# One factor of a state space layer, B a^r, made with the states on partitions and turned by TensorE; the loads of that layer put in another order

## The chip, the cores and the metric

The kernel runs on one core of a Trainium2 chip. The metric is device time in microseconds of one execution. Before the change three runs took 1512.39, 1514.38 and 1520.98 us, so the median is 1514.38 us.

## The reference

The program is a trunk of four residual layers on 256 tokens of 1024 channels, all in float32. Each layer is a token mixer, then cross-attention (4 heads) into 256 memory tokens, then a gated MLP (d_ff 2816) with a causal convolution of width 3. Layers 0 and 3 mix by trailing-window means, layer 1 by stick-breaking attention, layer 2 by a diagonal complex state space (64 groups of 16 channels, 64 complex states each) followed by a GLU. The part that matters here, cut:

```python
def s5_mixer(h, a_re, a_im, log_dt, b_re, b_im, c_re, c_im, d, w_glu):
    lam = lax.complex(a_re, a_im)
    dt = jnp.exp(log_dt)[:, None]
    a_bar = jnp.exp(lam * dt)
    b_bar = ((a_bar - 1.0) / lam)[..., None] * lax.complex(b_re, b_im)
    ...
    bu = jnp.einsum('bcgi,gpi->bcgp', u_blk, b_bar)          # u = rms_norm(h)
    xs = scan over the 256 tokens: x_t = a_bar x_{t-1} + bu_t
    y = jnp.real(jnp.einsum('bcgp,gip->bcgi', xs, c_mat)) + d * u
    val, gate = jnp.split(gelu(y) @ w_glu, 2, axis=-1)
    return val * sigmoid(gate)
```

## The kernel before, in words

All big products are three float32r matmuls on a high and a low part of each operand (`mm3`, L65 to L67). A weight tile of 1 MB is loaded on SyncE's queue into one of three `raw` buffers (L88), rounded to its high part `whi` by ScalarE (L70), and its rest `wlo` is formed by VectorE (L71), or by GpSimd where asked for. The MLP takes 22 chunks of 128 columns (`up0` to `up21`): 48 matmuls into `u`, the convolution on ScalarE and VectorE (L1251, L1253), a gate, and 12 matmuls into four accumulators `acc`, two chunks late.

The state space layer cuts the 256 tokens into 32 chunks of 8. It needs three tables that depend on parameters alone, and these are made long before layer 2, in gaps of earlier layers: `B a^r` for r = 0..7, by which eight inputs become one chunk's contribution to the state (`blD`, 8 blocks m of 128 x 1024, in DRAM); `C a^r`, by which a carried state becomes eight outputs (`caD`); and the taps inside a chunk, `C a^r B` (`tD`). In layer 2, `u` (the normed input) is reshuffled by eight DMAs into `uc` with the chunks on partitions, copied into `ur` in another order, transposed by TensorE into `v`, and multiplied with `bl` (from `blD`) into `S`. `S` is transposed to `SX`, VectorE scans over the chunks into `X` (L1053 to L1066), and TensorE adds the taps (`tu` from `tD`, L1078) and the carried states (`ou` from `caD`, L1098) into `Y`. After a GELU come the GLU's products. Between these steps stand units of the cross-attention's projections of the memory, k1, k2, k3, v0 and v1, which do not depend on the layer's input.

How `B a^r` is made before: `s5_rows` (L801) orders the powers `pr`, `pi` and the matrix `bb` on GpSimd, transposes them on TensorE and writes them as rows to DRAM (`pwD`, `bbD`) from ScalarE's queue. `s5_rows_in` (L832) reads for each block m one row for 16 partitions (powers) or 8 (matrix), twice 512 KB, on GpSimd's queue. `s5_ba` (L839) makes the complex product in six VectorE operations on 128 x 512 elements, already in the layout of `blD`, and GpSimd's queue writes the block. Blocks 0 to 4 stand in the MLP of layer 0 (chunks up7 to up21), blocks 5 to 7 in the stick-breaking attention of layer 1 (its heads 3 to 13), where all three write the same half of a tile `s5o`.

What sets the order: the code is written with `fill("name")` points; `run` puts pieces of other work there with `put` and `plan`. The build then orders each engine's instructions by its own schedule, under the data dependences and the `behind(...)` constraints. Each engine takes its instructions in that order, and one that waits holds up all behind it; each DMA queue is issued in order as well.

Of the kernel before, what the change touches and what calls it, by code (L numbers as in the profile page):

```python
# [8 lines left out]
F32 = mybir.dt.float32  # L9
# [5 lines left out]
P = 128  # L15
# [21 lines left out]
class Trunk:  # L37
# [684 lines left out]
    def s5_start(self):  # L722

        nc, v, a = self.nc, self.nc.vector, self.a
# [64 lines left out]

        self.pwD = self.dram.tile([8, 8, 1024], F32, name="pwD")  # L790
        self.bbD = self.dram.tile([8, 16, 1024], F32, name="bbD")
# [9 lines left out]
    def s5_rows(self, after):  # L801

        nc = self.nc
        pr, pi, bb, C, t1, t4, t5, t6 = self.s5p
        jobs = []
        for x, y in enumerate((pr, pi)):

            src = t4[:, 1536 + 256 * x : 1792 + 256 * x]
            with self.behind(*after):
                nc.gpsimd.tensor_copy(src.rearrange("p (m k q) -> p m k q", m=8, k=8), y[:, 0:8, :].rearrange("p k (q m) -> p m k q", m=8))  # L810
            jobs += [(src[:, h * P : (h + 1) * P], self.pwD[4 * h : 4 * h + 4], x) for h in range(2)]
        for x in range(2):

            src = t6[:, 512 * x : 512 * (x + 1)]
            bv = bb.rearrange("p (q m) x j -> p m x j q", m=8)[:, :, x]
            with self.behind(*after):
                nc.gpsimd.tensor_copy(src.rearrange("p (m j q) -> p m j q", m=8, j=16), bv)
            jobs += [(src[:, h * P : (h + 1) * P], self.bbD[2 * h : 2 * h + 2], x) for h in range(4)]
        for b in range(3):
            ps = self.bank()  # L820
            for i in range(4):
                src = jobs[4 * b + i][0]
                nc.tensor.transpose(ps[:, i * P : (i + 1) * P], src, self.ident[:])
            st = t4[:, 512 * b : 512 * (b + 1)]
            nc.scalar.copy(st, ps[:])
            for i in range(4):
                _, dst, x = jobs[4 * b + i]
                nc.scalar.dma_start(
                    dst.rearrange("m k (x q p) -> x (m k) q p", x=2, q=4)[x], st[:, i * P : (i + 1) * P]
                )  # L830

    def s5_rows_in(self, m, t):  # L832

        nc = self.nc
        w, b = self.pwD[m], self.bbD[m]
        nc.gpsimd.dma_start(t[:, 0:1024], bass.AP(tensor=w.tensor, offset=w.offset, ap=[[1024, 8], [0, 16], [1, 1024]]))
        nc.gpsimd.dma_start(t[:, 1024:2048], bass.AP(tensor=b.tensor, offset=b.offset, ap=[[0, 8], [1024, 16], [1, 1024]]))

    def s5_ba(self, m, t, of, tmp, x):  # L839

        v = self.nc.vector
        f = lambda t: t.rearrange("p (x q k) -> p x q k", x=2, q=4)
        w, b = f(t[:, 0:1024]), f(t[:, 1024:2048])
        o = of.rearrange("p (q x k) -> p q x k", q=4, x=2)
        tmp = tmp.rearrange("p (q k) -> p q k", q=4)
        v.tensor_mul(o[:, :, x], w[:, 0], b[:, x])
        v.tensor_mul(tmp, w[:, 1], b[:, 1 - x])
        (v.tensor_add if x else v.tensor_sub)(o[:, :, x], o[:, :, x], tmp)
        if x:
            self.nc.gpsimd.dma_start(self.blD[:, m, :], of)  # L850

    def s5_tiles(self, m):

        pr, pi, bb, C, t1, t4, t5, t6 = self.s5p
        return (t5 if m % 2 else t4), (t1 if m % 2 else t6)[:, 0:1024], t6[:, 1280:1792]

    def s5_tiles_later(self, m):

        if self.s5r is None:
            self.s5r = [self.kv.tile([P, 2048], F32, tag=t, name="s5r") for t in ("mgh", "mgl")]  # L860
            self.s5r.append(self.big.tile([P, 2048], F32, tag="xs", name="s5o"))
        o = self.s5r[2]
        return self.s5r[m % 2], o[:, 0:1024], o[:, 1024:1536]
# [75 lines left out]
    def s5_mixer(self, l, sp):  # L939
# [10 lines left out]
        land(1)  # L950
# [6 lines left out]
        chain, firsts, last = [], [None, None], None  # L957
        for tt in range(TT):
            r = rs[tt]
            for nh, f in enumerate((nc.vector.tensor_scalar_mul, nc.scalar.mul)):  # L960
                s = slice(512 * nh, 512 * (nh + 1))
                done = f(u[:, tt, s], self.h[:, tt, s], r[:, 0:1])
                firsts = firsts[1:] + [done.ins]

                for q in (2 * nh, 2 * nh + 1):
                    at = 32 * q + 16 * tt
                    queue = nc.scalar if nh else nc.sync
                    moved = queue.dma_start(
                        uc[at : at + 16].rearrange("c t a j -> c t (a j)"), u[:, tt, 256 * q : 256 * (q + 1)]
                    )  # L970
                    last = last if nh else moved
# [5 lines left out]
        db = sp.tile([P, 2, 256], F32, name="db")  # L977
        for i, row in enumerate((a["s5_d"][0], a["mix_norm_g"][l])):
            for q in range(4):
# [444 lines left out]
```

## Time and profile before

| what | value |
|---|---|
| median of the runs | 1514.38 us |
| the profiled execution: its time, its span | 1520.19 us, 1518.5 us |
| PE busy | 1440.2 us, 95% of the span |
| MLP of layer 0 | about 143 to 353 us |
| stick-breaking attention of layer 1 (projections and heads) | about 353 to 488 us |
| MLP of layer 1 | about 611 to 809 us |
| state space layer | about 809 to 950 us |
| MLP of layer 2, of layer 3 | about 1021 to 1209, 1320 to 1508 us |

TensorE is busy nearly always, so what the change is worth is read from the stretches where it is not, or where its clock was lowered, and from the instructions that it gains. The places that it touches are the MLP of layer 0, the attention of layer 1 and the state space layer.

### The profile page before, as it was taken

The numbers are of one execution on the slowest core, as the hardware profiler recorded it, in microseconds if no ns is written. First come the engines' busy times: TensorE is split into PE (matmuls) and PEld (weight loads), VectorE is DVE, ScalarE is ACT, GpSimd is POOL, SyncE is SP. The second block draws the span as 40 slices with busy tenths as digits, with TensorE's granted clock in tenths as the row PEclk, the third lists the DMA queues.
The fourth block names the chain that finished last, engine by engine and source line by source line (L and its number), as shares of the span: only waits on it lengthen the run. The fifth ranks groups of instructions, "written<-read, shape, count | busy, mean of one in ns | idle before, by whom it ended". The sixth has DMA issues, their size and how long they took to land.

```text
span 1518.5 us, 25333 instructions
## 1 busy us (share of the span) xinstructions
PE 1440.2 (95%) x10318; PEld 1324.3 (87%) x10318; DVE 1096.0 (72%) x1720; ACT 833.4 (55%) x1338; POOL 139.6 (9%) x148
## 2 busy tenths in 40 slices
PE   7999998899899999999997779999999999999997
PEld 7898997798898998999986667989999999899996
DVE  6868677678787666998874755768777686677775
ACT  6554543465677455655544334656555575465553
POOL 3401000000000000011113420000000030000000
PEclk9999999999899999999998889999999999999999
DMA  7567898655543555676577575536564455365551
GB/s 251 202 182 222 230 260 226 203 169 177 156 139 112 165 182 175 226 240 224 194 245 214 206 266 180 181 111 222 187 202 167 155 196 190 113 224 190 169 192 43
DMA packets 211737, 288.10 MB, mean 190 GB/s; under 512 B 26340, under 2 KB 167268, under 8 KB 209700
## 3 DMA queue, kind: packets, MB, share of 16 engines
q1 hardware_dynamic: 198820, 261.74, 52.5%
q0 software_dynamic: 10496, 23.43, 5.8%
q10 hardware_dynamic: 2304, 1.31, 0.4%
q8 instruction: 81, 1.33, 0.4%
q14 instruction: 36, 0.29, 0.1%
HBM read 271.81 MB, written 17.73 MB: 191 GB/s over the span
## 4 chain that ended last, share of the span: by engine, by line
PE 77%; DVE 10%; DMA 8%; issue 2%; ACT 2%; ACTq 0%; SPq 0%; POOL 0%; DVEq 0%; POOLq 0%
PE u L65 9%; PE u L66 9%; PE u L67 9%; PE mm L65 7%; PE acc L67 7%; PE acc L66 7%; PE mm L66 7%; PE acc L65 7%; PE mm L67 7%; DMA raw<-in_ffn_w_up_dram 4%; DVE wlo L71 3%; DVE ug L1253 1%; DMA raw<-in_xa_wkv_dram 1%; PE z L551 1%; DMA blD<-s5o 1%
## 5 line engine op out<-in xcount | busy, mean ns | idle before, releaser
L71 DVE TENSOR_TENSOR wlo<-raw,whi 128x1024 fp32r<-128x1024 f32 x428 | 517.8, 1221 | 181.0 <-ACT whi L70 163.0
L70 ACT CAST whi<-raw 128x1024 fp32r<-128x1024 f32 (+1 forms) x450 | 458.7, 1045 | 231.1 <-DMA raw<-in_ffn_w_up_dram 99.4
L65 PE MATMUL u<-ah,whi 128*128 128x256 f32 x1408 | 400.2, 284 | 2.9 <-DVE ug L1253 2.2
L67 PE MATMUL u<-ah,wlo 128*128 128x256 f32 x1408 | 399.8, 284 | 1.4 <-DVE wlo L71 1.4
L66 PE MATMUL u<-al,whi 128*128 128x256 f32 x1408 | 399.8, 284 | 0.2 <-DVE al L71 0.2
L65 PEld LDWEIGHTS u<-ah,whi 128*128 128x128 f32 x1408 | 271.2, 193 | 7.9 <-issue 3.6
L66 PEld LDWEIGHTS u<-al,whi 128*128 128x128 f32 x1408 | 271.2, 193 | 3.4 <-DVE al L71 0.7
L67 PEld LDWEIGHTS u<-ah,wlo 128*128 128x128 f32 x1408 | 271.1, 193 | 2.0 <-DVE wlo L71 2.0
L1253 DVE SCALAR_TENSOR_TENSOR ug<-u,cwT,ug 128x255 f32<-128x255 f32 x352 | 168.1, 480 | 86.4 <-ACT ug L1251 81.8
L1251 ACT ACTIVATE ug<-u,cwT 128x256 f32<-128x256 f32 x176 | 99.0, 563 | 159.4 <-PE u L67 86.6
L65 PE MATMUL acc<-whi,gg 128*128 128x512 f32 x352 | 140.0, 398 | 11.2 <-ACT gg L70 11.0
L66 PE MATMUL acc<-wlo,gg 128*128 128x512 f32 x352 | 139.5, 396 | 0.0
L67 PE MATMUL acc<-whi,gg 128*128 128x512 f32 x352 | 138.6, 395 | 0.7 <-DVE gg L71 0.6
L66 PE MATMUL mm<-al,whi 128*128 128x256 f32 x384 | 110.0, 287 | 0.1
L65 PE MATMUL mm<-ah,whi 128*128 128x256 f32 x384 | 110.1, 287 | 0.0
L67 PE MATMUL mm<-ah,wlo 128*128 128x256 f32 x384 | 109.7, 286 | 0.0
L176 POOL TENSOR_TENSOR r<-v,mhalf 128x1 f32<-128x1 f32 x28 | 21.0, 751 | 842.0 <-DVE v L172 673.0
L65 PEld LDWEIGHTS acc<-whi,gg 128*128 128x128 f32 x352 | 67.2, 191 | 23.9 <-ACT gg L70 12.2
L67 PEld LDWEIGHTS acc<-whi,gg 128*128 128x128 f32 x352 | 67.0, 190 | 17.2 <-DVE gg L71 2.7
L66 PEld LDWEIGHTS acc<-wlo,gg 128*128 128x128 f32 x352 | 67.3, 191 | 11.0
L66 PEld LDWEIGHTS mm<-al,whi 128*128 128x128 f32 x384 | 74.8, 195 | 0.8 <-DVE al L71 0.6
L65 PEld LDWEIGHTS mm<-ah,whi 128*128 128x128 f32 x384 | 75.0, 195 | 0.1
(354 smaller groups left out, 2605.0 us busy)
## 6 DMA issues: line engine op xcount, KB each, us to landing
raw<-in_ffn_w_up_dram SPq DMA_DIRECT2D x88, 1024.0 KB
raw<-in_ffn_w_down_dram SPq DMA_DIRECT2D x44, 1024.0 KB
raw<-in_xa_wkv_dram SPq DMA_DIRECT2D x30, 1024.0 KB
raw<-in_xa_wq_dram SPq DMA_DIRECT2D x16, 1024.0 KB
raw<-in_xa_wo_dram SPq DMA_DIRECT2D x16, 1024.0 KB
raw<-in_sb_w_qkv_dram SPq DMA_DIRECT2D x12, 1024.0 KB
raw<-in_s_w_glu_dram SPq DMA_DIRECT2D x8, 1024.0 KB
raw<-in_sb_w_o_dram SPq DMA_DIRECT2D x4, 1024.0 KB
```

What stands on the lines that cost most here:

```text
L65: mm(out, lh, rh, start=start, stop=False)
L66: mm(out, lh, rl, start=False, stop=False)
L67: self.multiplied = mm(out, ll, rh, start=False, stop=stop).ins
L70: x = self.nc.scalar.copy(hi, src)
L71: y = (eng or self.nc.vector).tensor_sub(lo, src, hi.bitcast(F32))
L176: self.powed = nc.gpsimd.tensor_tensor(r[:], v[:], self.mhalf[:], ALU.pow).ins
L551: mm(out, qk[a][rows, 4 + qc, ks], qk[b][rows, qc, :], start=kt == 1 and n == 0, stop=False, skip_group_check=True)
L1251: nc.scalar.activation(u[:, s, :], out, AF.Identity, bias=cw[3], scale=cw[2])
L1253: nc.vector.scalar_tensor_tensor(u[:, s, sh:], out[:, : T - sh], cw[2 - sh], u[:, s, sh:], ALU.mult, ALU.add)
```

## The change

First, `B a^r`. `s5_rows` and `s5_rows_in`, the DRAM tables `pwD` and `bbD`, the twelve transposes that made them, their twelve DMA writes from ScalarE's queue, four GpSimd copies and the sixteen reads of 512 KB are gone. `s5_ba` makes the same six products with the states on partitions, out of `pr`, `pi` and `bb` where they lie, through broadcast access patterns. The new `s5_turn` transposes the result on TensorE (eight 128 x 128 transposes a block), ScalarE copies two PSUM banks of 128 x 512 to SBUF, and GpSimd's queue writes the block to `blD` as before. Since `pr`, `pi` and `bb` have left SBUF by layer 1, one load of 800 KB (`s5r<-keepD`, on SyncE's queue) brings them back for blocks 5 to 7. The transposed blocks of layer 1 now alternate between two halves of `s5o`.

Second, layer 2. Only `land(0)` stands ahead of the eight `uc` DMAs, which all go on SyncE's queue (before, four went on ScalarE's); the loads of `db` are two instead of eight and stand behind them, and so do `land(1)` and `land(2)`. `ur` is allocated ahead of `v`. The first quarter of the taps (`taps_u(0)`) stands ahead of v1, the other three, with their loads, behind it; the loads `ou` take other buffers.

```diff
-    def s5_rows(self, after):
...
-    def s5_rows_in(self, m, t):
...
+    def s5_ba(self, m, where, x):
+        v = self.nc.vector
+        (pr, pi, bb), o, tmp, _ = where
+        sh = [P, 4, 8, 16]
+        w = [y.rearrange("p k (q m) -> p m q k", m=8)[:, m, :, 0:8].unsqueeze(3).to_broadcast(sh) for y in (pr, pi)]
+        bv = bb.rearrange("p (q m) x j -> p m q x j", m=8)[:, m]
+        b = [bv[:, :, i, :].unsqueeze(2).to_broadcast(sh) for i in range(2)]
+        f = lambda t: t.rearrange("p (q r j) -> p q r j", q=4, r=8)
+        o = o.rearrange("p (q x k) -> p q x k", q=4, x=2)[:, :, x].rearrange("p q (r j) -> p q r j", r=8)
+        v.tensor_mul(o, w[0], b[x])
+        v.tensor_mul(f(tmp), w[1], b[1 - x])
+        (v.tensor_add if x else v.tensor_sub)(o, o, f(tmp))
+    def s5_turn(self, m, where):
+        _, o, _, of = where
+        for b in range(2):
+            ps = self.bank()
             for i in range(4):
+                s = slice(512 * b + P * i, 512 * b + P * (i + 1))
+                nc.tensor.transpose(ps[:, P * i : P * (i + 1)], o[:, s], self.ident[:])
+            nc.scalar.copy(of[:, 512 * b : 512 * (b + 1)], ps[:])
+        nc.gpsimd.dma_start(self.blD[:, m, :], of)
...
     def s5_tiles_later(self, m):
         if self.s5r is None:
+            k, t = [self.kv.tile([P, 2048], F32, tag=t, name="s5r") for t in ("mgh", "mgl")]
+            self.nc.sync.dma_start(k[:, 0:1600], self.keepD[:, 0:1600])
...
+        k3, o, tmp, of = self.s5r
+        return k3, o, tmp, of[:, 1024 * (m % 2) : 1024 * (m % 2) + 1024]
...
         land(0)
-        land(1)
...
-                for q in (2 * nh, 2 * nh + 1):
-                    at = 32 * q + 16 * tt
-                    queue = nc.scalar if nh else nc.sync
-                    moved = queue.dma_start(
...
+            for q in range(4):
+                at = 32 * q + 16 * tt
+                last = nc.sync.dma_start(
...
+        db = sp.tile([P, 2, 256], F32, name="db")
         with self.behind(last.ins):
+            for i, row in enumerate((a["s5_d"][0], a["mix_norm_g"][l])):
+                nc.sync.dma_start(db[:, i, :], bass.AP(tensor=row.tensor, offset=row.offset, ap=[[256, 4], [0, 32], [1, 256]]))
+            land(1)
             land(2)
...
-        v = self.acts.tile([P, 16, P], F32, tag="ah", name="v")
         ur = self.acts.tile([P, 16, 8, 16], F32, tag="ah", name="ur")
+        v = self.acts.tile([P, 16, P], F32, tag="ah", name="v")
...
+        taps_land(0)
...
         self.late = steps[-1:]
+        taps_u(0)
         self.fill("scan1")
         self.late = ()
+        for mm in (1, 2, 3):
+            landed = taps_land(mm)
+            taps_u(mm)
         def carry(mm):
-            pool, tag = ((self.big, "xs"), (self.acts, "ah"), (self.raw, "raw"), (self.raw, "raw"))[mm]
+            pool, tag = ((self.big, "xs"), (self.raw, "raw"), (self.raw, "raw"), (self.acts, "ah"))[mm]
...
+        for m in range(8):
+            l, tiles, at = (0, self.s5_tiles, [f"up{4 + 3 * m + i}" for i in range(3)])
+            if m > 4:
+                l, tiles, at = (1, self.s5_tiles_later, [f"head{1 + 4 * (m - 5) + i}" for i in (1, 2, 3)])
+            for x in range(2):
+                put((l, at[x]), lambda m=m, tiles=tiles, x=x: self.s5_ba(m, tiles(m), x))
+            put((l, at[2]), lambda m=m, tiles=tiles: self.s5_turn(m, tiles(m)))
+        put((1, "head0"), lambda: self.s5_tiles_later(5))
```

The schedule moves more than the diff shows. On VectorE, at the start of layer 1 (`al` is the normed input's low part, `s5o` and `s5r` belong to `B a^r`, `L` to the attention's first head), before:

```order
L71 TENSOR_TENSOR al<-mm,ah 128x4x128 x2
L846 TENSOR_TENSOR s5o<-s5r 128x4x128
L847 TENSOR_TENSOR s5o<-s5r 128x512
L846 TENSOR_TENSOR s5o<-s5r 128x4x128
L71 TENSOR_TENSOR wlo<-raw,whi 128x1024 x4
L71 TENSOR_TENSOR al<-mm,ah 128x512
L71 TENSOR_TENSOR wlo<-raw,whi 128x1024 x2
L848 TENSOR_TENSOR s5o<-s5o 128x4x128
L847 TENSOR_TENSOR s5o<-s5r 128x512
```

On the same engine at the same place, after the change:

```order
L71 TENSOR_TENSOR al<-mm,ah 128x4x128 x2
L71 TENSOR_TENSOR wlo<-raw,whi 128x1024 x4
L71 TENSOR_TENSOR al<-mm,ah 128x512
L71 TENSOR_TENSOR wlo<-raw,whi 128x1024 x4
L71 TENSOR_TENSOR al<-mm,ah 128x512
L558 TENSOR_SCALAR L<-z 128x384
L559 TENSOR_TENSOR L<-L,ab 128x384
```

No product of `B a^r` is left there: the six of block 5 stand in the last chunks of layer 0's MLP, the others further into the heads. Likewise the six of block 0 moved forward, into the norm ahead of layer 0's MLP, between the residual adds (L434) and the scaling of its second half (L248).

On SyncE's queue, from the load of k3's weights to the last load of `bl` (`db` is a small table for the skip term; lines of the change are some 26 lower):

```order
 L88 DMA raw<-in_xa_wkv_dram 128x8x256
-L980 DMA db<-in_s_d_dram 32x256 x4
-L980 DMA db<-in_mix_norm_g_dram 32x256 x4
-L946 DMA bl<-blD 128x2048
-L968 DMA uc<-u 16x8x256 x4
-L946 DMA bl<-blD 128x2048
+L922 DMA bl<-blD 128x2048
+L943 DMA uc<-u 16x8x256 x8
+L952 DMA db<-in_s_d_dram 128x1x256
+L952 DMA db<-in_mix_norm_g_dram 128x1x256
+L922 DMA bl<-blD 128x2048 x2
```

The load of `bl` that waited behind the eight of `db` now follows k3's weights directly; two loads of `bl` stand behind the `uc` DMAs instead of one.

On the same queue, from v0's weights to the GLU's:

```order
 L88 DMA raw<-in_xa_wkv_dram 128x4x512 x2
-L1074 DMA tu<-tD 128x2048 x4
+L998 DMA tu<-tD 128x2048
 L88 DMA raw<-in_xa_wkv_dram 128x4x512 x2
-L1090 DMA ou<-caD 128x2048 x4
-L88 DMA raw<-in_s_w_glu_dram 128x4x512
+L998 DMA tu<-tD 128x2048 x3
+L1076 DMA ou<-caD 128x2048 x4
+L88 DMA raw<-in_s_w_glu_dram 128x4x512 x3
```

Three of the four loads of taps moved behind v1's weights. The four `ou` stand in the order 0, 3, 1, 2: `ou` 3 takes the buffer of the first taps, and `ou` 1 and 2 take the `raw` buffers of the second and third taps, so they wait until TensorE has used those. Before, one GLU load came ahead of the next layer norm's row, now three do.

More of the change, by code (lines that the diff above doesn't have):

```diff
@@ L788, in s5_start @@
         self.blD = self.dram.tile([P, 8, 1024], F32, name="blD")
-        self.pwD = self.dram.tile([8, 8, 1024], F32, name="pwD")
-        self.bbD = self.dram.tile([8, 16, 1024], F32, name="bbD")
         self.caD = self.dram.tile([P, 8, 8, P], F32, name="caD")
@@ L799, in s5_start @@
         )
-    def s5_rows(self, after):
-        nc = self.nc
[L804 to L819, printed above, removed]
+    def s5_ba(self, m, where, x):
[10 more added lines that the diff above has]
+        (v.tensor_add if x else v.tensor_sub)(o, o, f(tmp))
@@ L820, in s5_rows @@
+    def s5_turn(self, m, where):
+        nc = self.nc
+        _, o, _, of = where
+        for b in range(2):
             ps = self.bank()
             for i in range(4):
[L822 to L830, printed above, removed]
@@ L832, in s5_rows_in @@
-    def s5_rows_in(self, m, t):
[L834 to L850, printed above, removed]
+                s = slice(512 * b + P * i, 512 * b + P * (i + 1))
@@ L859, in s5_tiles_later @@
         if self.s5r is None:
[L860 to L863, printed above, removed]
+            k, t = [self.kv.tile([P, 2048], F32, tag=t, name="s5r") for t in ("mgh", "mgl")]
+            self.nc.sync.dma_start(k[:, 0:1600], self.keepD[:, 0:1600])
+            f = lambda n: k[:, n : n + 288].rearrange("p (k g) -> p k g", k=9)
@@ L865, in s5_back @@
+            k3 = f(0), f(288), k[:, 576:1600].rearrange("p (g x j) -> p g x j", x=2, j=16)
+            self.s5r = k3, t[:, 0:1024], t[:, 1024:1536], self.big.tile([P, 2048], F32, tag="xs", name="s5o")
+        k3, o, tmp, of = self.s5r
+        return k3, o, tmp, of[:, 1024 * (m % 2) : 1024 * (m % 2) + 1024]
     def s5_back(self):
@@ L956, in s5_mixer @@
         uc = sp.tile([P, 8, 16, 16], F32, name="uc")
-        chain, firsts, last = [], [None, None], None
+        chain, firsts = [], []
         for tt in range(TT):
             r = rs[tt]
+            firsts = []
             for nh, f in enumerate((nc.vector.tensor_scalar_mul, nc.scalar.mul)):
@@ L1017, in s5_mixer, with taps_land @@
         self.fill("s")
+        tus = []
+        def taps_land(mm):
+            pool, tag = ((self.acts, "ah"), (self.raw, "raw"), (self.raw, "raw"), (self.raw, "raw"))[mm]
+            tu = pool.tile([P, 2, 2, 4, P], F32, tag=tag, name="tu")
+            tus.append(tu)
+            return nc.sync.dma_start(tu[:].rearrange("p r m q k -> p r (m q) k"), self.tD[mm]).ins
+        taps_land(0)
         SX = self.acts.tile([P, NCH, 2, GP], F32, tag="al", name="SX")
@@ L1068, in s5_mixer, with taps_u @@
         self.fill("scan0")
-        values = self.multiplied
         Y = self.accs()
-        for mm in range(4):
-            tu = self.raw.tile([P, 2, 2, 4, P], F32, tag="raw", name="tu")
-            landed = nc.sync.dma_start(tu[:].rearrange("p r m q k -> p r (m q) k"), self.tD[mm]).ins
-            with self.behind(values):
+        def taps_u(mm):
+            with self.behind(self.multiplied):
                 for m, par, q in [(m, par, q) for m in (2 * mm, 2 * mm + 1) for par in range(2) for q in range(4)]:
@@ L1332, in run @@
         put((0, "fnorm"), self.s5_start)
-        put((0, "up3"), lambda: self.s5_rows(self.transposed_all))
-        early = lambda m, x: self.s5_ba(m, *self.s5_tiles(m), x)
-        for m in range(2):
-            put((0, f"up{4 + m}"), lambda m=m: self.s5_rows_in(m, self.s5_tiles(m)[0]))
-        for m in range(5):
-            at = 7 + 3 * m
-            put((0, f"up{at}"), lambda m=m: early(m, 0))
-            put((0, f"up{at + 1}"), lambda m=m: early(m, 1))
-            if m < 3:
-                put((0, f"up{at + 2}"), lambda m=m: self.s5_rows_in(m + 2, self.s5_tiles(m)[0]))
-        later = lambda m, x: self.s5_ba(m, *self.s5_tiles_later(m), x)
-        for m in (5, 6, 7):
-            at = 3 + 4 * (m - 5)
-            put((1, f"head{at - 2 if m < 7 else at - 1}"), lambda m=m: self.s5_rows_in(m, self.s5_tiles_later(m)[0]))
-            put((1, f"head{at}"), lambda m=m: later(m, 0))
-            put((1, f"head{at + 2}"), lambda m=m: later(m, 1))
+        for m in range(8):
[6 more added lines that the diff above has]
+        put((1, "head0"), lambda: self.s5_tiles_later(5))
         put((1, "up0"), self.s5_back)
```

16 lines of the change are left out of this document (6 added, 10 removed).

## The prediction

> **What bounds the kernel now.** I read the chain of waits first, by engine and by line.
>
> ```profile
> PE 77%; DVE 10%; DMA 8%; issue 2%; ACT 2%; ACTq 0%; SPq 0%; POOL 0%; DVEq 0%; POOLq 0%
> ```
>
> TensorE sets the end; what the change can win lies in the DMA share. So the busy times of the stretches came next: the four MLPs, layer 1's start, its heads, and the head of the state space layer (columns as the first line says).
>
> ```profile
> core 0: us, PE busy (x) PEld busy (x) DVE busy (x) ACT busy (x) POOL busy (x), PEclk, DMA share, GB/s
> 143.00:353.00 210.00, 196.21 (x1329) 180.82 (x1329) 149.86 (x234) 105.08 (x160) 14.79 (x24) 0.97 0.74 217
> 611.00:809.00 198.00, 195.82 (x1604) 181.44 (x1603) 164.88 (x253) 109.01 (x177) 26.45 (x30) 1.00 0.69 227
> 1320.00:1508.00 188.00, 187.54 (x1317) 176.62 (x1316) 134.12 (x200) 105.14 (x155) 0.00 (x0) 0.99 0.49 166
> 353.00:395.00 42.00, 34.67 (x243) 31.04 (x243) 31.02 (x44) 25.29 (x45) 3.32 (x5) 0.93 0.63 172
> 395.00:488.00 93.00, 93.00 (x619) 84.45 (x618) 72.72 (x119) 71.53 (x140) 1.08 (x2) 0.96 0.38 127
> 814.00:832.00 18.00, 8.12 (x66) 7.92 (x66) 2.42 (x4) 4.09 (x6) 8.62 (x21) 0.83 1.03 248
> ```
>
> One MLP costs 188 us undisturbed (the third row); the first, where `B a^r` is made, takes 210, so 22 more. Its waits say why: first ScalarE's in the first MLP, then the same line in the third (1020 to 1207), then rows of the chain there and at the state space layer.
>
> ```profile
> ACT whi L70 <- DMA raw<-in_ffn_w_up_dram: 48.0, 8, 10.0
> ```
>
> ```profile
> ACT whi L70 <- DMA raw<-in_ffn_w_up_dram: 8.0, 7, 1.4
> ```
>
> ```profile
> 181.62 12.76 DMA raw<-in_ffn_w_up_dram
> ...
> 231.93 12.70 DMA raw<-in_ffn_w_up_dram
> ...
> 822.43 8.41 DMA uc<-u
> ...
> 893.39 3.15 issue
> ```
>
> Weights come late by 48.0 us in all, against 8.0 in an MLP with nothing beside it. Beside it run the reads that spread rows of `pwD` and `bbD` over the partitions, two of 512 KB for each of the eight blocks (`s5_rows_in`), on GpSimd's queue; the group of the first three from `bbD`:
>
> ```profile
> s5d<-bbD POOLq DMA_DIRECT2D x3, 512.0 KB, 9.7
> ```
>
> **Part one: `B a^r` by transposes.** The prices come from the rows of the old code that do the same things, and from one VectorE product whose operand is broadcast:
>
> ```profile
> L823 PE MATMUL mm<-ident,s5f x8: 272/272/273, 165.6 to 166.4; 128*128 128x128 f32 x8
> L825 ACT COPY s5d<-mm x3: 575/588/596, 167.4 to 174.0; 128x512 f32<-128x512 f32 x3
> L846 DVE TENSOR_TENSOR s5f<-s5d x6: 679/682/684, 198.5 to 260.9; 128x512 f32<-128x512 f32 x6
> 120.49 0.68 DVE L662 TENSOR_TENSOR s5b<-poles,s5a 128x512 f32<-128x512 f32 x1
> ```
>
> Eight transposes start within 0.8 us, seven steps of 0.11. Removed: twelve transposes, three copies, and sixteen reads of 512 KB, 8.4 MB. Added: 64 transposes and 16 copies, one load of 800 KB. The 48 products stay; in the new access pattern no row has them, only the 0.68 of the broadcast one, so I keep 0.68, with 0.6, since nothing excludes a small gain, and 1.28 (what 1024 elements take at L187, quoted below) as ends; beside the MLP VectorE has 60 us to spare either way.
>
> *First MLP.* Five blocks turn there: 40 x 0.11 = +4.4 on PE. The copies, 10 x 0.59 = 5.9, hide in ScalarE's 105 busy of 210, unless ScalarE is the late one; then they cost their 5.9. With ten reads gone, about 5 MB, the up weights should be nearly on time. One load comes into SyncE's queue instead, `s5r`, between two of the ninth chunk's up loads; it waits for block 3's write to land, since its buffer is only read after that, and all weights behind it wait too, as do block 5's products at the MLP's end if it lands late, and the splits of weights behind those on VectorE. On GpSimd's queue only further writes stand behind the new ones. I charge 4 for that and for the eight writes to `blD` that stay, with 0 and 12 (one of the four waits above) as ends. So 22 − 4.4 − 4 = 13.6 saved, between 18 and 6: **−13.5**.
>
> *The norm before it.* Block 0's six products now stand on VectorE between the residual adds and the scaling, on the way to the MLP:
>
> ```profile
> 135.05 0.21 DVE L172 TENSOR_SCALAR v<-ss 128x1 f32<-128x1 f32 x1 [0.79 <-ACT acc L157]
> 135.94 1.28 DVE L187 SCALAR_TENSOR_TENSOR xs<-h,r,xs 128x1024 f32<-128x1024 f32 x1 [0.68 <-POOL r L176]
> 138.80 0.69 DVE L434 TENSOR_TENSOR h<-h,acc 128x512 f32<-128x512 f32 x1 [0.84 <-PE acc L67]
> 141.16 0.84 DVE L248 TENSOR_SCALAR xs<-xs,r 128x512 f32<-128x512 f32 x1 [0.67 <-POOL r L176]
> ```
>
> Six at 0.68 are 4.1; idle time of 0.79 + 0.68 + 0.84 + 0.67 = 3.0 lies there, of which I let two thirds, 2.0, be filled: **+2.1** (six at 0.6 with all 3.0 filled: 0.6; at 1.28, with 3.0 filled: 4.7).
>
> *Layer 1's start.* In the old order VectorE waits there for a write to `blD` that still reads `s5o`, and the first head's work stands behind it:
>
> ```profile
> 387.94 0.69 DVE L846 TENSOR_TENSOR s5o<-s5r 128x512 f32<-128x512 f32 x1 [7.26 <-DMA blD<-s5o]
> 389.15 0.45 PE L566 MATMUL z<-Ll,tri 128*128 128x384 f32 x1 [1.06 <-DVE Ll L71]
> 393.49 0.69 PE L566 MATMUL z<-Lh,tri 128*128 128x384 f32 x1 [2.45 <-ACT Lh L70]
> 394.62 0.69 PE L566 MATMUL z<-Ll,tri 128*128 128x384 f32 x1 [0.44 <-DVE Ll L71]
> ```
>
> Both go: the product to the end of the MLP, the wait with the alternating halves of `s5o`. PE's three waits are 4.0 us, and the clock of 0.93 in this stretch may lengthen some 15 us after them by 7%, 1.0: **−5** (−2, if `Lh` is late from the weight splits alone, to −8, nearly the 7.3 between 42.00 and 34.67).
>
> *The heads.* Blocks 5 to 7 turn beside them, where PE has no gap (93.00 of 93.00): 24 x 0.11 = **+2.6**; with nothing overlapped 24 x 0.27 = 6.5. The copies and products fit beside 71.5 and 72.7 of 93.
>
> The Trainium skill, page "TensorE: Matmul & The Clock Gate", section "Part 4: PE-mode transpose", speaks against this part: it gives about 275 ns to a transpose in one kernel's context, most of it access latency. At that price for each the sum would be rival C's. The row's 272 ns agrees as the duration of one, but its eight starts in 0.8 us contradict it as the price of one in a row of them.
>
> **Part two: the state space layer.** These rows, of the timeline and one group (the four loads of taps), carry it:
>
> ```profile
> 814.78 3.22 SPq L968 DMA_DIRECT2D uc<-u  x4
> 813.35 9.65 ACTq L968 DMA_DIRECT2D uc<-u  x4
> 831.54 3.67 PE L998 MATMUL mm<-ident,ur 128*128 128x128 f32 x16 [9.88 <-ACT ur L994]
> 835.14 4.22 PE L1012 MATMUL mm<-bl,v 128*32 128x128 f32 x128
> 861.62 2.83 PE L1078 MATMUL acc<-tu,v 128*32 128x128 f32 x96
> L1074 SPq DMA_DIRECT2D tu<-tD x4: 319/328/339, 839.4 to 862.8; - x4
> 867.71 1.93 PE L1078 MATMUL acc<-tu,v 128*32 128x128 f32 x32 [3.26 <-DMA tu<-tD]
> 877.02 1.36 PE L65 MATMUL mm<-whi,mgh 128*128 128x512 f32 x2 [7.38 <-DVE two L1064]
> 889.86 3.52 PE L1098 MATMUL acc<-ou,X 64*32 64x128 f32 x236
> 899.83 0.80 PE L65 MATMUL mm<-whi,ah 128*128 128x512 f32 x1 [1.31 <-ACT ah L1118]
> ```
>
> PE idles 9.88 us for `uc`. ScalarE gave out its four loads over 9.65 us, the last near 822.4, and it landed 8.41 later, amid 1.03 of the DMA engines. SyncE takes 3.22/4 = 0.8 an issue: eight from 813.3 end by about 819.7, three earlier, with less traffic ahead of them (two `db` loads for eight and one `bl` for two). The gain is 3 if the landing keeps its 8.41 and up to 9.9 if the gap closes. I take 5, for a second wait stands behind it: `land(1)` and `land(2)` now follow `uc`, with some 3 MB ahead of or among them at 248 GB/s, 12 us from 820, so the third quarter of the 128 matmuls with `bl` (835.14 + 4.22/2 = 837.3 before) can't start ahead of 832.
>
> With 5 the scan ends at 872. v1's matmuls (12.84 from 877.02 to 889.86) run to 885. Now the new wait: three quarters of the taps (0.03 each, 0.94 a quarter) stand behind v1, and `ou` 1 and 2 take the buffers of two of them. `ou` 1 goes out at 886; a 1 MB load took 4.9 (tap load 862.8, used 867.7): 891. `ou` 2, behind it, at 1 MB/248 GB/s = 4.2 more: 895.2. Two quarters of the carry remain, 128 x 0.015 = 1.9: 897.1; the old one, after its 3.15 of "issue" from 893.39, ended there too. Behind `ou` on SyncE's queue come the GLU's first weights, formerly long in place: issued near 887, landed near 899, cast and split by 901. The GLU starts at 901, not 899.83: **+1**, between −6 (neither wait bites) and +5 (`uc` gains nothing and `ou` waits).
>
> **Sum.** −13.5 + 2.1 − 5 + 2.6 + 1 = −12.8. The profiled execution took 1520.19, 5.8 above the median of 1514.38; 1507.4 in its terms, **1501.6** in the median's.
>
> **Rivals**, with times in the median's terms.
>
> *A, all of the state space gain stays.* If `land(2)` and `ou` are on time, the GLU starts 5.5 earlier instead of 1 later: −19.3, 1495.1. For it: the old carry waited 3.15 on nothing seen, so my sum there may be too strict. Against: the buffers of `ou`.
>
> *B, the weights stay late.* Writes to `blD` and `s5r`'s place in SyncE's queue hold the weights back, and the first MLP goes to 203 only: −13.5 becomes −5, the sum −4.3: 1510.1. For it: layer 1's MLP, with none of these reads, is at 198 too. Against: it makes tables of its own.
>
> *C, transposes at full price.* If they don't overlap among other matmuls, each of 52 more costs 0.16 on top: +8.4, the sum −4.4: 1510.0. Against: the row of eight, with its 0.11; for it: they follow matmuls of another kind here, whose weights are loaded ahead. The rule of the Trainium skill named above would give this time.
>
> *D, slower: every turn stalls PE's order.* A turn needs two of four PSUM banks and ScalarE's two copies, which stand in order behind a cast that waits for weights: 48.0/8 = 6.0 us a time. Five turns stop PE by 6 each in the first MLP: +30, a sum of +17.2, 1531.6. It decides from 12.8/8 = 1.6 us a turn on. For it: both engines run in order, and PE's own next matmul stands behind the transposes. Against: the wait that it multiplies is the one that the change should shorten, and the first pair of transposes finds its banks free.
>
> **How the numbers follow.** Forecast 0.48, A 0.18, B 0.20, C 0.05, D 0.09. A change under 0.5% is about what cannot be told from none here: faster is below 1506.8, slower above 1522.0. The forecast's own range, 1495 to 1508, gives 0.43 faster, 0.05 same; A 0.18 faster; B 0.05, 0.14 and 0.01 slower; C 0.01 and 0.04; D 0.02 same, 0.07 slower: 0.67, 0.25, 0.08. The range takes in A, B and C with their spread, 1488 to 1515, and leaves out most of D.
>
> **What would show it.** Right: the first MLP at 193 to 200 us and ScalarE's wait for up weights under 20; transposes spaced 0.11; no wait of VectorE on `blD` after 353; PE's gap before the `ur` transposes under 6, then a wait on `bl` inside the 128; a wait of PE or the carry on `ou` after v1, and GLU weights as the last to come. Wrong: the 48.0 reappearing as waits behind `s5r`; PE idle ahead of or after the new transposes; the norm's products longer than 0.68; a GLU start that keeps all of the gain.

## The result

The changed kernel took 1501.86 us (median of four, 1500.12 to 1504.49), the kernel before on the same chip 1515.52 (1512.39 to 1520.98): a ratio of 0.9908, 95% interval 0.9887 to 0.9928, so some 14 us faster. The prediction said 1501.6. The profiled execution of the change has a span of 1502.8 us, against 1518.5, 15.7 less; that is 2 us more than the medians differ, since the one execution of the kernel before lay 4.7 above its median and that of the change 2.6 above its own. The stages, each from its first TensorE instruction to that of the next, show that this sum is made of larger pieces of both signs:

| stage, in the profiled executions | predicted | measured |
|---|---|---|
| before the norm ahead of the first MLP | 0 | −1.7 |
| that norm | +2.1 | +1.5 |
| first MLP | −13.5 | −18.7 |
| layer 1's start and its heads | −2.4 | −5.3 |
| layer 1's cross-attention and MLP | 0 | +1.4 |
| state space layer, up to the GLU's first matmul | +1 | +4.1 |
| the GLU, up to the next layer's norm | 0 | +2.8 |
| the rest | 0 | +0.1 |
| sum | −12.8 | −15.7 |

How far such a difference can be trusted is seen from the kernels of the experiments below. Layer 1's MLP up to the first `uc` load, which no edit of theirs touches but in the order of the loads at its end, took 196.4 to 203.5 us in their profiles, so the +1.4 means nothing. The first MLP took 195.5 to 198.1 in the seven kernels that have the change's, and 214.3 and 221.7 in the two that have the old one: its gain is clear, its size is not to a microsecond.

Busy times by stretch, first of the kernel before: its first MLP, the start of layer 1, layer 1's heads with what follows them up to the next norm, the state space layer from its first `uc` load, and its GLU.

```profile
core 0: us, PE busy (x) PEld busy (x) DVE busy (x) ACT busy (x) POOL busy (x), PEclk, DMA share, GB/s
143.46:357.78 214.32, 197.57 (x1334) 181.74 (x1333) 153.73 (x240) 108.92 (x175) 14.89 (x25) 0.97 0.73 213
357.78:375.10 17.32, 16.91 (x126) 15.71 (x126) 16.32 (x21) 13.21 (x17) 2.15 (x3) 0.90 0.62 200
375.10:501.69 126.59, 122.63 (x789) 109.73 (x788) 92.62 (x148) 86.47 (x163) 2.25 (x4) 0.96 0.46 140
813.35:899.83 86.48, 60.18 (x766) 51.48 (x764) 43.90 (x69) 26.45 (x36) 33.76 (x34) 0.83 0.72 230
899.83:948.29 48.46, 47.02 (x201) 38.55 (x201) 29.70 (x33) 24.92 (x30) 0.00 (x0) 0.95 0.64 212
```

The same five of the change:

```profile
143.21:338.85 195.64, 192.61 (x1362) 181.07 (x1361) 156.47 (x238) 114.63 (x182) 4.75 (x8) 1.00 0.58 194
338.85:357.66 18.81, 18.23 (x125) 17.06 (x125) 13.47 (x16) 13.32 (x17) 0.87 (x1) 0.82 0.63 210
357.66:477.48 119.82, 119.82 (x813) 108.31 (x813) 92.33 (x146) 90.18 (x169) 2.23 (x4) 1.00 0.41 135
...
790.38:881.19 90.81, 61.63 (x767) 53.05 (x766) 44.00 (x69) 27.07 (x37) 34.03 (x34) 0.85 0.70 221
881.19:932.44 51.25, 47.90 (x201) 38.78 (x202) 30.05 (x33) 24.63 (x30) 0.00 (x0) 0.93 0.61 200
```

In the MLP TensorE's idle time fell from 16.7 to 3.0 us, and the granted clock rose from 0.97 to 1.00. The heads have no idle time left (119.82 of 119.82) where they had 4.0, again at 1.00 instead of 0.96. The waits in the MLP of the change (ScalarE) and the chain of waits (eight transposes a block) say the same:

```profile
ACT whi L70 <- DMA raw<-in_ffn_w_up_dram: 10.5, 9, 2.3
```

```profile
189.99 0.88 PE mm L820 x8
216.36 0.87 PE mm L820 x8
```

ScalarE's 48.0 us of waiting for up weights became 10.5, and TensorE waits for none of them: its 3.0 us of idle time are one wait at the norm behind the MLP, which the kernel before has too. Eight transposes take 0.88 us, 0.11 each, with no wait on them.

The state space layer went the other way. The waits of TensorE there in the change, then three rows of its chain and one of SyncE's queue, and the stretch behind v1's weights:

```profile
PE mm L65 <- DVE vl L71: 12.3, 1, 12.3
PE acc L1084 <- DMA ou<-caD: 4.9, 2, 2.7
PE mm L972 <- ACT ur L968: 4.5, 1, 4.5
PE mm L986 <- DMA bl<-blD: 4.5, 2, 4.0
...
PE acc L65 <- ACT whi L70: 1.9, 1, 1.9
```

```profile
798.61 15.73 DMA bl<-blD
...
867.37 9.68 DMA raw<-in_s_w_glu_dram
...
886.49 7.66 DMA raw<-in_s_w_glu_dram
```

```profile
839.98 26.84 SPq L1076 DMA_DIRECT2D ou<-caD  x4
```

```profile
852.00:867.00 15.00, 15.00 (x140) 12.40 (x144) 6.45 (x11) 1.18 (x2) 0.00 (x0) 0.90 0.05 9
```

The gap before the `ur` transposes fell from 9.88 to 4.5, but a wait of 4.5 on `bl` came behind it. The longest wait, 12.3, is v1's first matmul behind the scan on VectorE, where the split `vl` that it waits for now stands ahead of the last steps; before, all four quarters of the taps and waits of 3.3 and 7.4 us lay between v0 and v1. Later SyncE's four `ou` issues stretch over 26.84 us, since two of them wait for buffers that the late taps hold. Nothing behind them is loaded: from 852 to 867 the DMA engines move 9 GB/s. The GLU's weights are then the last to come, twice on the chain, and TensorE waits 1.9 us for one of them (`acc`, the last row of the first list).

### The profile page after: what moved, and what is told of

It reads as the page before. It is cut to its first block, busy times and chain, and to the rows that moved or that the text cites. A ratio compares the mean times of both kernels' runs of the same rounds, so it can differ in the third digit from the quotient of the medians.

```text
span 1502.8 us, 25420 instructions
## 1 busy us (share of the span) xinstructions
PE 1436.3 (96%) x10370; PEld 1325.5 (88%) x10370; DVE 1100.1 (73%) x1720; ACT 843.0 (56%) x1351; POOL 127.1 (8%) x128
## 4 chain that ended last, share of the span: by engine, by line
PE 75%; DVE 12%; DMA 7%; ACT 3%; issue 2%; SPq 0%; POOL 0%; DVEq 0%; POOLq 0%; ACTq 0%
PE u L66 9%; PE u L67 9%; PE u L65 9%; PE mm L66 7%; PE mm L65 7%; PE mm L67 7%; PE acc L66 6%; PE acc L65 6%; PE acc L67 6%; DMA raw<-in_ffn_w_up_dram 3%; DVE wlo L71 3%; DVE ug L1239 2%; ACT whi L70 1%; DMA raw<-in_s_w_glu_dram 1%; DMA bl<-blD 1%
## 5 line engine op out<-in xcount | busy, mean ns | idle before, releaser
L65 PE MATMUL acc<-whi,gg 128*128 128x512 f32 x352 | 138.0, 392 | 0.0
L67 PE MATMUL acc<-whi,gg 128*128 128x512 f32 x352 | 136.9, 389 | 0.0
```

What stands on the lines that cost most here:

```text
L65: mm(out, lh, rh, start=start, stop=False)
L67: self.multiplied = mm(out, ll, rh, start=False, stop=stop).ins
```

## The experiments

All ratios are to the kernel before, on the same chip in the same rounds; the change itself has 0.9908 (0.9887 to 0.9928). A thousandth is 1.5 us.

### The two parts apart

`ba_only` is the change with the old function `s5_mixer`:

```diff
         land(0)
+        land(1)
...
-                last = nc.sync.dma_start(
+                    queue = nc.scalar if nh else nc.sync
+                    moved = queue.dma_start(
...
-        for mm in (1, 2, 3):
-            landed = taps_land(mm)
-            taps_u(mm)
```

> Only part one (B a^r by transposes); the state space layer as in the kernel before. Theory: part one gives all of the gain and part two costs some 6 us, so this is faster than the whole change: the first MLP at about 196 us, layer 1's MLP begun some 24 us earlier than before, the stretch from the ur transposes to the next layer's norm as long as before (117 us), the total 18 to 24 us under the kernel before (about 1494). Rival: part two pays for itself, and the total is 10 to 14 us under the kernel before (about 1502) or less.

Measured: 1494.71 us, ratio 0.9839 (0.9818 to 0.9861). `s5_only` is the reverse, the kernel before with the change's `s5_mixer`.

> Only part two (the order in the state space layer); B a^r as in the kernel before. Theory: slower than the kernel before by 4 to 8 us (1519 to 1523): the gap before the ur transposes halves, a wait on bl of about 4 us and waits on ou of about 5 us come instead, and the GLU starts 3 to 6 us later in relation to the end of layer 1's MLP. Rival: 1 to 5 us faster than before, since uc lands 9 us earlier.

Measured: 1528.39 us, ratio 1.0055 (1.0032 to 1.0078). −16.1 and +5.5 thousandths add to −10.6, and the change has −9.2 (−11.3 to −7.2), so the parts hardly act on each other. Part one carries the whole gain, part two costs a third of it or more: by `s5_only` 5.5 thousandths, by the change against part one alone 6.9. The profile of `s5_only` is the weaker witness of the two: its state space layer and GLU are 7.5 us longer than in the kernel before, but so is its first MLP, by 7.4, where nothing was changed. In the profile of part one alone the state space layer and its GLU are shorter even than in the kernel before, 84.20 + 47.43 us (before: 86.48 + 48.46, the change: 90.81 + 51.25):

```profile
792.19:876.39 84.20, 58.99 (x766) 51.08 (x764) 42.97 (x69) 26.21 (x35) 33.72 (x34) 0.86 0.71 228
876.39:923.82 47.43, 45.55 (x200) 36.73 (x200) 29.93 (x32) 24.89 (x30) 0.00 (x0) 1.00 0.69 232
```

The code is the same there as in the kernel before; the difference is mostly the gap before the `ur` transposes, 7.2 instead of 9.9.

### Where part two loses

`taps_early` moves three quarters of the taps, with their loads, back ahead of v1:

```diff
         taps_u(0)
+        for mm in (1, 2, 3):
+            landed = taps_land(mm)
+            taps_u(mm)
         self.fill("scan1")
         self.late = ()
-        for mm in (1, 2, 3):
-            landed = taps_land(mm)
-            taps_u(mm)
```

> The whole change, but all four quarters of the taps ahead of v1, with their loads, as in the kernel before; the buffers of ou stay. Theory: the loss of the change after the scan comes from ou 1 and 2 and the GLU's weights queueing for buffers that the late taps hold; with the taps in the scan's shadow the DMA engines no longer stand idle there (15 us at 9 GB/s in the change), the waits on ou shrink from 4.9 us to under 1.5, and the total falls 5 to 8 us below the change (about 1495). Rival: the waits move to v1's weights, which now stand behind more loads, and the total stays within 2 us of the change.

Measured: 1498.5 us, 0.9866 (0.9851 to 0.9881). Faster than the change, by 6.4 us going by the ratios and by 3.4 going by the medians, where 5 to 8 were expected. Its profile shows where. No wait on `ou` is left, and the GLU takes 47.6 us instead of 51.3; in the fourteen profiles it takes 47.4 to 48.5 in the five kernels whose taps all stand ahead of v1, and 49.5 to 51.9 in the nine others. Up to the GLU's first matmul nothing is gained (91.6 us from the first `uc` issue, the change 90.8). The carry does end 4.1 us earlier, 83.7 after that issue, although a first quarter of it now stands ahead of v1 and waits 14.9 us for the scan; but behind it TensorE waits 2.3 us for the GELU and 4.6 for the GLU's input `ah`, where the change has no wait and one of 1.7. `land1_first` puts the second `bl` load back ahead of `uc`:

```diff
         land(0)
+        land(1)
...
-            land(1)
             land(2)
```

> The whole change, but land(1) stands ahead of the uc loads again, as in the kernel before; everything else of part two stays. Theory (part two's opening gives its gain back because the second bl load lies behind uc): TensorE's wait on bl in the 128 matmuls falls from 4.5 us to under 1, they end 3 to 4 us earlier in relation to the first uc issue, and the total is 2 to 4 us under the change (about 1498 to 1500). Rival (the later waits on ou and the GLU's weights absorb it): within 1 us of the change.

Measured: 1502.02 us, 0.9906 (0.9872 to 0.9940), no gain that the times can show. Its profile does show the mechanism: the 128 matmuls with `bl` end 23.1 us after the first `uc` issue instead of 27.5, and the wait on `bl` falls from 4.5 to 1.9. The GLU begins 88.2 us after the first `uc` issue, where the change and the seven other kernels with its order have 89.4 to 92.4. `both_mended` makes both edits.

> land1_first and taps_early in one kernel: uc on one queue and the new buffers stay, land(1) ahead of uc, all taps ahead of v1. Theory (these two orders are what part two loses by): the two gains add, 3.4 + 3 us, and the total comes to that of part one alone or below, 1492 to 1496. Rival (a third thing in part two costs as much, for instance that the first quarter of the carry now stands ahead of v1 on TensorE and waits for the scan there): 1497 or more.

Measured: 1495.59 us, 0.9860 (0.9821 to 0.9899). From the first `uc` issue to the next layer's norm, the profiles have 142.1 us in the change, 139.2 with the taps moved, 139.5 with `land(1)` moved, 135.2 with both, 134.9 in the kernel before and 131.6 in part one alone. So the two orders are what part two loses against the kernel before, 6.9 of 7.1 us; together they bring more than the 2.9 and 2.5 of each alone. The total is within the theory's 1492 to 1496, and by the ratios, whose intervals overlap, it can't be told from part one alone; in the profiles the stretch is still 3.6 us behind it, all of it ahead of the GLU. The two profiles that share the old order differ by 3.3 there, so even this is not settled. TensorE's largest wait is at the place that the rival named, where a first quarter of the carry stands ahead of v1:

```profile
PE acc L1084 <- POOL wlo L71: 15.3, 1, 15.3
...
PE mm L65 <- ACT ah L1104: 4.5, 2, 3.8
PE yt L1101 <- ACT uc L1095: 2.3, 1, 2.3
```

The first row names `wlo`, which the carry doesn't read; the scan's last step ended at 851.9, and the carry began at 852.0. But this wait is not where the 3.6 us lie: the whole carry ended 80.6 us after the first `uc` issue, in part one alone 81.2. They lie behind it, as in `taps_early`: TensorE waits 2.3 for the GELU and 3.8 for `ah`; part one alone has no wait at the first and 2.0 at the second. On VectorE and ScalarE splits and casts of weights stand there ahead of the GELU and of `ah`, and one cast waits 2.0 us for a GLU load. That this order is the cause was not tried.

`uc_sp` takes part one alone and adds only what part two promised at its opening:

```diff
-                    queue = nc.scalar if nh else nc.sync
+                    queue = nc.sync
...
-                    last = last if nh else moved
+                    last = moved
...
+        db = sp.tile([P, 2, 256], F32, name="db")
         with self.behind(last.ins):
+            for i, row in enumerate((a["s5_d"][0], a["mix_norm_g"][l])):
+                nc.sync.dma_start(db[:, i, :], bass.AP(tensor=row.tensor, offset=row.offset, ap=[[256, 4], [0, 32], [1, 256]]))
             land(2)
-        db = sp.tile([P, 2, 256], F32, name="db")
-        for i, row in enumerate((a["s5_d"][0], a["mix_norm_g"][l])):
-            for q in range(4):
...
```

> Part one alone, with one piece of part two: all eight uc loads on SyncE's queue and the two db loads behind them; two bl loads stand ahead of uc, as before. Theory (uc's earlier landing is a gain as long as bl is not put behind it): PE's gap before the ur transposes 2 to 4 us shorter than the 7.2 of part one alone, no wait on bl, total 1.5 to 3 us under part one alone (about 1492). Rival (the transfers share the DMA engines, and only the landing of the last matters): within 1 us of part one alone.

Measured: 1491.54 us, 0.9839 (0.9813 to 0.9866), the same ratio as part one alone; by the times the two can't be told apart. The profile speaks for a small gain in the place itself: 80.17 us from the first `uc` issue to the GLU instead of 84.20 (86.48 in the kernel before, with the same order), the gap before `ur` 5.7 instead of 7.2, less than the 2 to 4 expected, and no wait on `bl`:

```profile
789.36:869.53 80.17, 60.93 (x768) 51.91 (x767) 44.02 (x69) 26.61 (x36) 33.95 (x34) 0.85 0.74 228
```

Both kernels beat the change.

### What made the first MLP long

Three kernels put ten reads of 512 KB of the old form back beside the change's MLP, on GpSimd's queue. `reads_back` issues two for each block into a tile of the MLP that is free:

```diff
+        def reads(m):
...
+                self.nc.gpsimd.dma_start(t[:, 1024 * i : 1024 * i + 1024], src)
...
+        for m in range(5):
+            put((0, f"up{4 + 3 * m}"), lambda m=m: reads(m))
```

> The whole change, with ten broadcast reads of 512 KB added in the first MLP on GpSimd's queue, in the pattern and at about the places of the old ones, into a buffer that nothing reads. Theory: the first MLP was long because the reads delayed the up weights; it goes from 195.6 us to 203 to 210, ScalarE's wait for up weights there back over 30 us, the total to about 1510 to 1516. Rival: the saving came from the work around the reads (VectorE products that waited for them, the rows' transposes and their copies), and the MLP stays within 3 us of 195.6, the total at about 1502.

Measured: 1522.64 us, 1.0028 (1.0011 to 1.0044). Far more than expected, but in the wrong place: the reads had nothing to wait for but each other and ran ahead of the MLP, which began at 159.9 us instead of 143.2, since the norm's `r` stood behind them on GpSimd's queue. The MLP itself was only 4.4 us longer. `reads_paced` therefore writes them over each block once TensorE has transposed it.

```diff
         nc.gpsimd.dma_start(self.blD[:, m, :], of)
+        for i in range({0: 3, 1: 2, 2: 3, 4: 2}.get(m, 0)):
...
+            nc.gpsimd.dma_start(o[:, 0:1024], src)
```

> The whole change, with ten broadcast reads of 512 KB again, but each held back until TensorE has transposed the block whose buffer it overwrites (three behind block 0, two behind 1, three behind 2, two behind 4), so that none runs in the norm ahead of the MLP. Theory (the reads delay the up weights): the first MLP goes from 195.6 us to 201 to 208 and ScalarE's wait for up weights there from 10.5 us to over 30; the total to about 1508 to 1514. Rival (the norm was the whole cost of the ten reads that ran early, and inside the MLP the DMA engines have room): MLP within 3 us of 195.6, total within 4 us of the change.

Measured: 1527.14 us, 1.0079 (1.0054 to 1.0105), the MLP 218.8. That is above both expectations, and again for a cause of the experiment's own: the products of blocks 2 and 4 now wait on VectorE until the reads have landed, with the weights' splits behind them.

```profile
DVE s5d L808 <- DMA s5d<-in_ffn_w_up_dram: 22.3, 2, 11.5
```

`reads_clean` lets them go into memory that no other engine reads or writes; a copy of two elements on GpSimd holds each pair back until its turn is done.

```diff
         nc.gpsimd.dma_start(self.blD[:, m, :], of)
+        if m < 5:
+            nc.gpsimd.tensor_copy(t[:, 1023:1025], of[:, 1022:1024])
...
+                nc.gpsimd.dma_start(t[:, 1024 * i : 1024 * i + 1024], src)
```

> The whole change, with ten broadcast reads of 512 KB, two behind each of the first MLP's five turns, into a buffer that no product and no engine touches, so that nothing but the DMA engines is shared (a copy of two elements on GpSimd holds each pair back until its turn is done). Theory (contention in the DMA engines alone delays the up weights): MLP 200 to 208 us instead of 195.6, ScalarE's wait for up weights over 25 us instead of 10.5, total 1507 to 1514. Rival (what the reads cost in the kernel before is the waiting of the products and turns on them, as reads_paced showed for VectorE; their transfers fit beside the weights): MLP under 199, total within 4 us of the change.

Measured: 1509.63 us, 0.9950 (0.9929 to 0.9971), 6 to 8 us above the change. The MLP took 203.2 instead of 195.6, and ScalarE's wait for up weights rose from 10.5 to 25.9:

```profile
ACT whi L70 <- DMA raw<-in_ffn_w_up_dram: 25.9, 8, 6.4
```

No other engine waits for these reads, so that transfers alone can delay the weights is shown: by 7.6 us in the MLP for ten reads. Some 1.3 of them lie ahead of the first read, at 194 us (a wait of 0.5 at 143, and half clock for 3.4 us of the MLP's start instead of 1.9), which leaves 6.3; the ratios give 6.4. `rows_back` puts the other removed step back, `s5_rows` with its twelve DMAs on ScalarE's queue.

```diff
+        put((0, "up3"), lambda: self.s5_rows(self.transposed_all))
```

> The whole change, with the old step s5_rows put back into the first MLP (four GpSimd copies, twelve transposes, three ScalarE copies and twelve DMAs of 64 KB on ScalarE's own queue) into memory that nothing reads; none of the broadcast reads comes back. Theory (the reads' contention, 7.6 us for ten in reads_clean, isn't all of the first MLP's saving; the rest was ScalarE held up by issuing and waiting for these twelve DMAs, from 167 to 181 us in the kernel before): the MLP 4 to 9 us longer than 195.6, total 1505 to 1510. Rival (ScalarE has time to spare, and the saving beyond the reads came from the products no longer waiting for them): MLP within 2 us of 195.6, total within 2 us of the change.

Measured: 1506.87 us, 0.9935 (0.9905 to 0.9965), the MLP 201.9 us. Of its 6.3 more, most is not what the step cost in the kernel before. TensorE ran at half its clock from 140.6 to 150.8, for 7.6 us of the MLP instead of 1.9, worth 2.8. It waited 1.5 us at 144 for `al`: the step's GpSimd copies ran there, and beside them two of block 0's products took 1.55 us each on VectorE instead of 0.68; the kernel before has no products there. The twelve transposes, at 168, are 1.3. ScalarE does wait for the twelve DMAs, as it did in the kernel before (3.6 and 3.3 us there):

```profile
ACT ug L1270 <- DMA bbD<-s5a: 5.7, 1, 5.7
```

But this reaches TensorE in one wait of 0.8 us at 181; the kernel before has two there, 1.3 in all. So the step was worth some 2 to 3 us with its transposes, and in the times the intervals of this kernel and of the change overlap.

What the 18.7 are made of can also be read from the two profiles directly. TensorE's idle time fell by 13.7. Half clock fell from 13.5 us of the MLP to 1.9, worth up to 5.8 (last section). The 28 transposes more cost 28 x 0.11 = 3.1. That makes 16.4 and leaves 2.3 open. In the kernel before, all of TensorE's waits in the MLP but the one at the norm lie between 180 and 295 us, and the reads were issued from 174.6 to 274.7: fourteen, not ten, since those of blocks 5 and 6 began there too. At 6.3 for ten, fourteen come to 8.8, an estimate; with the rows that is about half of the 21.8 that the MLP gained before it paid for the transposes. Why the old reads cost more than those of `reads_clean` was not tried; they came in closer order, fourteen in 100 us against ten in 117.

### The price of a turn

`turns_twice` makes each block's transposes and copies twice:

```diff
-        for b in range(2):
+        for b in (0, 1, 0, 1):
```

> The whole change, with the transposes and copies of every block done twice: 64 more transposes and 16 more copies. Theory (a transpose costs TensorE its spacing, 0.11 us, and ScalarE's copies hide): 64 x 0.11 = 7.0 us more, total about 1509, half of it or more in the first MLP. Rival (each costs its whole 0.27): 17.4 us more, about 1519. Rival (a turn stops TensorE's order behind ScalarE's copies, 1.6 us or more each time): 13 us or more on top of the 7, with idle time of PE at the new transposes.

Measured: 1515.24 us, 0.9984 (0.9961 to 1.0007), some 11 to 13 us above the change: between the first theory (7.0) and the others. The chain has sixteen transposes in 1.75 us, 0.11 each, so the price per transpose holds; layer 1's start and heads grew by 3.4, near 24 x 0.11 = 2.6. The MLP grew by 11.6, and only 4.4 of that are transposes:

```profile
144.26:351.53 207.27, 200.54 (x1401) 187.44 (x1401) 156.86 (x238) 119.30 (x192) 3.93 (x8) 0.98 0.54 183
306.20:312.90 6.70, 5.78 (x27) 5.71 (x27) 3.25 (x4) 3.34 (x7) 0.53 (x1) 0.50 0.36 118
```

Idle time rose from 3.0 to 6.7 us, and 6.8 us at half clock followed from 306 on, worth 3.4: 4.4 + 3.7 + 3.4 are the whole. TensorE waited 2.8 us at the doubled transposes, for ScalarE's copies and VectorE, and 0.9 right behind them. So the stall of rival D exists, but far below 1.6 us a turn. `one_half` undoes the alternating halves of `s5o`.

```diff
-        return k3, o, tmp, of[:, 1024 * (m % 2) : 1024 * (m % 2) + 1024]
+        return k3, o, tmp, of[:, 0:1024]
```

> The whole change, but the blocks of layer 1 all use one half of s5o, as the kernel before did. Theory as predicted (the alternating halves take the wait on the write to blD away): a wait of 4 us or more at layer 1's copies or products comes back, and the total is 2 to 5 us above the change. Rival (the turns stand 28 us apart now and a write lands in 4 to 10, so nothing waits; it was moving block 5's products out of layer 1's start that counted): the total within 1 us of the change.

Measured: 1502.38 us, 0.9913 (0.9892 to 0.9935), as the change. No engine waits on the write to `blD` in its layer 1 either. The halves did nothing. That leaves the other two things that changed there, which were not tried apart: the turns stand 28 us apart, and block 5's products left layer 1's start.

## Why the prediction was right, and where it was not

The time came out within a microsecond, and the mechanism of its largest term held; but the closeness is partly luck. The two early stages gained 8 us more than predicted and the state space layer and its GLU lost 6 more, and the prediction carried the whole 5.8 by which the profiled execution lay above its median over to the changed kernel, whose own lay 2.6 above.

**First MLP, −13.5 against −18.7.** The cause was right: the weights came late because of the reads. The sign to look for was ScalarE's wait under 20 us, and it is 10.5. The saving lies just outside the stated 18 to 6. What was mis-sized is the charge of 4 for `s5r` and the writes to `blD`: the waits for up weights lie 2.5 above the 8.0 of an undisturbed MLP, and none reaches TensorE. The transposes cost the 4.4 that the sum had, but twelve old ones, 1.3, went in return and were not counted. The reads that went were fourteen, not ten, and TensorE's clock, which has a part in the 22 us, was not named.

**The norm, +2.1 against +1.5.** As sized.

**Layer 1, −5 + 2.6 against −5.3.** The 4.0 us of waits went, as the sum had it. The clock's share was put at 1.0 and was several times that, since 0.93 is the mean of a stage with 10 us at half clock in it. They began within the longest of those waits, at 392.5:

```profile
392.60:402.70 10.10, 8.76 (x35) 7.92 (x36) 10.06 (x18) 9.06 (x19) 0.48 (x1) 0.50 0.65 208
```

Half of that is 5 us, and it is gone: 119.82 us at 1.00. The start itself became 1.5 us longer, with half clock for 6.9 us instead of 3.4. Start and heads together took 136.7 to 139.5 us in the profiles of the kernels with the change's layer 1 (142.0 with the turns doubled), and 143.9 and 143.0 in the two with the old one. The step "the wait with the alternating halves" was wrong (`one_half`): it goes without them.

**The state space layer, +1 against +4.1.** Both new waits were foreseen, at the places named: on `bl` inside the 128 matmuls, and on `ou` after v1, with the GLU's weights as the last to come. Both were mis-sized. The term "I take 5" for `uc` was lost: the 128 matmuls with `bl` ended 27.5 us after the first `uc` issue (before: 26.0), and the scan, to end 5 earlier, ended 2.7 later. The step that "the third quarter can't start ahead of 832" took 3 MB at 248 GB/s for the landing of `bl`, 18.7 after the first `uc` issue; in the change that load took 15.73 us and landed 24.0 after it, where the third quarter stood before as well (835.14 + 2.1 against 813.35). v1 nevertheless ended 2.4 earlier, as the split that it waits for (`vl`) passed the scan's last steps on VectorE. Behind it came three quarters of the taps, 2.8 us that the scan had hidden before; the waits on `ou`, 4.9 instead of 3.15 of "issue"; and a carry partly at half clock. So the carry ended 3.9 us later in relation to the first `uc` issue, not at the same time. The −6 end of this term's range, and rival A with it, were out of reach in this order, though not in another: `uc_sp` is 6.3 us shorter up to the GLU than the kernel before.

**The GLU, 0 against +2.8.** This term was missing. The prediction counted the late weights only up to the GLU's first matmul; the next ones came late as well: the chain has them at 886.49, and 1.9 of the 2.8 are TensorE's wait for one. With all taps ahead of v1 the loss is gone (47.6 and 47.4 us in `taps_early` and `both_mended`).

**The rivals.** B fell (10.5 us instead of 48.0), C fell by the row of eight and by `turns_twice`, and D stalls TensorE in neither stretch of the change: its waits list shows none at the new transposes. (B's own sum has a slip: an MLP at 203 saves 7 of 210, not 5, so its time would be 1508.1.) The slower side did exist, though not as D: part two by itself is a slowdown of 0.55%, which the prediction carried only as a small term.

## What to carry to other kernels

A table that a kernel spreads over partitions by repeated reads can cost more than the wait for it: here the transfers delayed the weights that TensorE lives on (`reads_clean`). Turning it on TensorE cost 64 x 0.11 = 7 us, less than half of what the waits that went were worth. A load that was moved forward brought nothing where what the next step needs was moved behind it: list the arrivals that the first instruction and the one after it wait for. On a queue that issues in order, one load that waited for a late reader held up everything behind it, and part of its price appeared a stage later, here in the GLU. And work that was hidden behind a scan is paid for in full when it is moved out from there.

## What the runs showed of the hardware

TensorE's clock lengthened what short waits cost, and I had not expected its share. In the kernel before, a wait of 5.4 us in the first MLP (the longest of four on ScalarE's `gg`) runs into this stretch, and another of 3.4 us at half speed follows at 273:

```profile
249.20:255.90 6.70, 5.60 (x13) 4.14 (x14) 6.70 (x13) 2.87 (x6) 1.76 (x3) 0.50 0.58 196
```

The records of the clock know only full and half speed, in pieces of 3.4 us. The Trainium skill, page "TensorE: Matmul & The Clock Gate", section "What's actually happening", has these two states and a window of 3.4 us in which TensorE's activity is counted; the traces agree, with 0.50 in the stretches above and 1.00 in the change's MLP and heads. So the 4.0 us of waits at layer 1's start were worth about 4 + 5, and the 3.7 of more idle time in `turns_twice` 3.7 + 3.4. Not every wait is followed by such a stretch: after one of 2.7 us at 292 in the kernel before the clock stayed at 1.00. Where such a stretch falls differs between profiles of kernels that are alike there (3.4, 6.8 and 10.2 us at the start of the first MLP in the change, `one_half` and `rows_back`), so that a few microseconds between two profiled executions mean little without a timed comparison.
